# The second residual turned to token rows: 32x32 blocks on VectorE and DMAs of 128-byte runs in place of 32 transposes on TensorE

## The chip, the cores and the metric

One core of one Trainium2 chip runs the whole layer in one launch. The metric is the device time of one execution in microseconds (us), the median of the runs shown. A profile of one execution stands beside it; its span is counted from the first to the last instruction, and the positions in it (for example "at 508.29") are us from the start of the span.

The engines named below: PE is TensorE (PEld its weight loads), DVE is VectorE, ACT is ScalarE, POOL is GpSimd, SP is SyncE, which here only issues DMAs. A "q" behind an engine's name means its instruction queue.

## The reference

One macaron layer on x of 512 tokens by 1024 channels, all in float32:

```python
x = x + 0.5 * swiglu_ffn(rmsnorm(x, ffn1_norm), ffn1_w_gate, ffn1_w_up, ffn1_w_down)
x = x + hybrid_mixer(rmsnorm(x, mix_norm), w_in, q_norm, k_norm, rel_bias, pool_w, pool_scale, w_out)
x = x + 0.5 * swiglu_ffn(rmsnorm(x, ffn2_norm), ffn2_w_gate, ffn2_w_up, ffn2_w_down)
x = rmsnorm(x, final_norm)

def swiglu_ffn(x, w_gate, w_up, w_down):
    return (jax.nn.silu(x @ w_gate) * (x @ w_up)) @ w_down
```

The mixer is attention in chunks of 64 tokens and a pooling mixer side by side, then one output projection. The feed-forward width is 2816.

## The kernel before

**Number format.** Every matmul is done three times on float32r parts: an operand is split into a high part (a cast, mostly on ACT, line 130) and a low part (a subtraction on DVE, line 131). `mm3` (lines 183 to 188) multiplies high by high (L186), high by low (L187) and low by high (L188). Such a group of three matmuls is called a unit below.

**Layout.** Up to the end of the mixer, the residual is kept turned: `x[k]`, k from 0 to 7, is a tile of 128 channels by 512 tokens. The last block leaves its product by rows: 128 tokens by 512 channels. So the residual, as it stands after the mixer, is needed a second time, by rows of tokens, and is put aside in DRAM in between, in `x_d`: eight tiles (`half`, `t`) of 128 tokens by 512 channels.

**Stages.** First feed-forward block, mixer, second feed-forward block. The second one is `ffn_up` (gate and up projections), then the products of the down projection (`down2.product`). Of `ffn_up`, the first four of 22 blocks of 128 features are multiplied plainly (`PLAIN[1]` is 4), the others by a Strassen scheme with seven half-size products per block.

**The stage around the change** runs from about 480 to 570 in the span:

- The mixer ends with the output projection. `add_out(d)` (L1611, DVE) adds each of its eight column blocks to `x[d]`; `h_high`, `h_low` and `h_square` (L1620, L1629, L1640) split `x[d]` times the gain of the norm and square it; `h_sum` (L1645) adds the squares up in `acc`.
- Lines 1699 to 1708 then turn the residual: for each of the eight tiles of `x_d`, four transposes of 128x128 on PE (L1703) into one PSUM bank of the tag "a" (four banks), a copy to a tile `z` from the temporaries on ACT (L1707), and a store of 256 KB from SP (L1708).
- `ffn_up` begins with the first four blocks (two pairs of gate and up) at once: for each of four weight panels `wA[kp]` (512 KB, loaded by SP at L179 and split at L130 and L131) eight units, 32 in all, into four PSUM banks `first`. They are named kp0 to kp3 here. With the fourth panel comes `norm.finish`, at a raised priority: the sum of squares per token on PE (L304), root on ACT (L311), reciprocal on DVE, and the spread to all partitions on PE (L325), which ends in `rb` (L327, ACT).
- `evacuate` (L407 to L416) empties two of those banks: DVE multiplies the gate's bank by `rb` into a temporary `g` (L409), ACT takes the Silu into a temporary `sg` (L411), DVE multiplies by `rb` (L413) and by the up bank (L704).
- Then come the blocks of n = 2 and n = 3 (L506 to L542), 16 units each, and between them, in pieces, `norm.blocks`, which makes the operands of the Strassen products from `x` and `rb` on DVE and ACT (L350, L356, L133, L134). From L560 the order of PE, DVE and ACT is written out by hand.
- `make_sums` (L685 to L697) has POOL add weight blocks of the down projection in DRAM with DMAs (L694), a few for each block of features; each batch waits for a copy of a column that DVE has written (`mark`, L692). SP loads the first of these sums at L721.
- The rows of `x_d` are read back by `again` (L1713 to L1715), from 727.0 in the span on.

**What sets the order.** Outside the hand-written parts a planner at build time orders each engine's instructions by priority, which follows the order in the program, and puts an instruction of a later line into a gap of an earlier stage where its data and buffers are there. Each engine then runs its own list in that order. The mixer's end has an order of its own, planned by costs, but instructions of `ffn_up` can stand between it. The temporaries (`temp()`, tag "t") are eight buffers of 128x512 float32 for all users: `z`, `g`, `sg`, the squares and the diagonal of the norm.

Of the kernel before, what the change touches and what calls it, by code (L numbers as in the profile page):

```python
# [16 lines left out]
P = 128  # L17
D = 1024
S = 512
KD = D // P  # L20
NT = S // P
# [16 lines left out]
PLAIN = (5, 4)  # L38
# [16 lines left out]
def layer(  # L55
# [31 lines left out]
    nc = tc.nc  # L87
# [12 lines left out]
    def name(what):  # L100
        n_tiles[0] += 1
        return f"{what}_{n_tiles[0]}"

    def temp(dtype=F32):
        return tpool.tile([P, S], dtype, tag="t", name=name("t"))

    def bank(tag="mm", bufs=4):
        return ps.tile([P, S], F32, tag=tag, name=name(tag), bufs=bufs)

    def abank():  # L110
        return bank("a", 4)
# [61 lines left out]
    def weights(src, parts=1):  # L173
        n = src.shape[-1]
        raw = raw_tile()
        hi, lo = part_tiles()
        for i in range(parts):
            part = slice(i * n // parts, (i + 1) * n // parts)
            nc.sync.dma_start(raw[:, part], src[:, part])  # L179
            split(raw[:, part], hi[:, part], lo[:, part])  # L180
        return hi, lo

    def mm3(acc, a, b, start, stop, further=False):

        more = dict(skip_group_check=True) if further else {}
        nc.tensor.matmul(acc, a[0], b[0], start=start, stop=False, **more)  # L186
        nc.tensor.matmul(acc, a[0], b[1], start=False, stop=False, **more)  # L187
        nc.tensor.matmul(acc, a[1], b[0], start=False, stop=stop, **more)  # L188

    def cut(pair, lo, n):  # L190
        return pair[0][:, lo : lo + n], pair[1][:, lo : lo + n]


    def residual_tiles():
        pairs = [xpool.tile([P, 2 * S], F32, tag=f"x{k}", name=name("x")) for k in range(KD // 2)]
        return [pairs[k // 2][:, k % 2 * S : (k % 2 + 1) * S] for k in range(KD)]

    x = residual_tiles()
    x_d = dram.tile([2 * NT, P, S], F32, name="x_d")
# [3 lines left out]
    ident = const.tile([P, P], F32, name="ident")  # L203
# [190 lines left out]
            ]  # L394


    def ffn_up(norm, wA, down, loaded, in_order, plain):

# [6 lines left out]
        def evacuate(f, gate, up):  # L407
            g = temp()
            nc.vector.tensor_tensor(g, gate, norm.rb, op=ALU.mult)  # L409
            sg = temp()  # L410
            nc.scalar.activation(sg, g, AF.Silu)  # L411

            nc.vector.tensor_tensor(sg, sg, norm.rb, op=ALU.mult)  # L413
            down.place(f, up, sg)
            down.sums(f)
            return sg  # L416

        first = [bank() for _ in range(4)]
        for kp in range(KD // 2):
            if not loaded:  # L420
                load(2 * kp)
            w = weights(wA[kp], 1 if loaded or kp else 4)
            if not loaded:
                load(2 * kp + 1)
                norm.square(2 * kp)
                norm.square(2 * kp + 1)
            if kp == KD // 2 - 1:
                with tc.high_priority():
                    norm.finish()
            for kk in range(2):  # L430
                k = 2 * kp + kk
                for j in range(4):
                    mm3(first[j], cut(w, (kk * 4 + j) * P, P), norm.h[k], k == 0, k == KD - 1)
        evacuate(0, first[0], first[1])
        evacuate(1, first[2], first[3])
        aside = [
# [123 lines left out]
        with tc.manual_schedule(engines={E.PE, E.DVE, E.Activation}):  # L560
            last_silu = last_place = last_sums = nothing
            for n in range(plain, KF):
                f = down.order[n]
                acc, up_lo, up_hi = bank()[:, :HT], bank()[:, :HT], abank()[:, :HT]
                u, z, sg = temp(), temp(), temp()
# [71 lines left out]
    class Down:  # L637
# [76 lines left out]
        def load(self, room):  # L714

            if self.ahead:
                i, g = self.ahead.pop(0)
                raw = self.loaded[i, g] = room[:, :1024]
                src = self.rows(i, g)
                c = S if tuple(src.shape[1:]) == (groups[g][1], S) else groups[g][1] * P  # L720
                nc.sync.dma_start(raw.rearrange("p (n c) -> p n c", c=c), src)  # L721
                if room.shape[-1] > 1024:
                    self.load(room[:, 1024:])
# [85 lines left out]
    n1, n2, n3 = Norm(0), Norm(1), Norm(2)  # L809
# [19 lines left out]
    down2 = Down(list(range(KF)), lambda f: (f // 2, f % 2), block2)  # L829

    with tc.tile_pool(name="act1", bufs=1, reuse_waits="tile") as apool, ExitStack() as in_order:
        down1.begin(apool)
        ffn_up(n1, wA1, down1, False, in_order, PLAIN[0])
        x[:] = residual_tiles()
        for k in range(KD):
# [56 lines left out]
    with tc.tile_pool(name="mix", bufs=1, reuse_waits="tile") as mpool:  # L892
# [19 lines left out]
        def job(engine, cost, rank, emit, after=(), gets=(), uses=(), lag=0.0, chunk=None):  # L912
            z = Job(engine, cost, rank, emit, after, gets, uses, lag, chunk)
            z.waits = len(z.after)
            for other in z.after:
                other.then.append(z)
            for key in uses:
                held_by[key] = held_by.get(key, 0) + 1
            jobs.append(z)
            return z  # L920
# [12 lines left out]
        def part_at(slot):  # L933
# [4 lines left out]
            t=(8, lambda slot: temp()),  # L938
# [116 lines left out]
        def load_raw(i):  # L1055
            def emit():
                raw, src = buf["raw", i], sources[i]
                if len(src.shape) > 2:
                    to = raw.rearrange("p (i d k c) -> p i d k c", i=2, d=2, k=2)
                    for j in range(2):  # L1060
                        nc.sync.dma_start(to[:, j], src[:, j])
                else:
                    nc.sync.dma_start(raw, src)

            return emit
# [12 lines left out]
        for i in range(len(sources)):  # L1078
            z = job("sp", 0.4, i, load_raw(i), gets=[("raw", ("raw", i))], lag=2.0 if i < RAW else 3.6)
# [6 lines left out]
        for k, t in enumerate((7.2, 8.5, 9.7, 12.8)):  # L1086
            z = job("sp", 0.0, -9, None, lag=t)
# [46 lines left out]
        z = job("act", 1.8, -1, root_of, [z])  # L1134
        at_r = job("dve", 0.8, -1, reciprocal_root, [z], uses=["total"])
        z = job("dve", 0.65, -1, diagonal, [at_r], [("t", "diag")])
        z = job("pe", 0.9, -1, spread, [z], [("bank", "wide")], ["diag"])
# [48 lines left out]
        def pool_weights(part):  # L1186
            def emit():
                if not part:
                    w_pool.extend(
                        mpool.tile([P, S], F32R, tag=f"wp{i}", name=f"wp{i}") for i in range(2)  # L1190
                    )
                    nc.scalar.copy(w_pool[0], buf["wp"])
                else:
                    nc.vector.tensor_tensor(
                        w_pool[1], buf["wp"], w_pool[0].bitcast(F32), op=ALU.subtract
                    )

            return emit

        z = job("sp", 0.4, 5, lambda: nc.sync.dma_start(buf["wp"], wP), gets=[("t", "wp")], lag=3.6)  # L1200
        z = job("act", 0.6, RANK["wp"], pool_weights(0), [z, ready[3]])
# [407 lines left out]
        def add_out(d):  # L1609
            def emit():  # L1610
                nc.vector.tensor_tensor(x[d], x[d], buf["out", d], op=ALU.add)  # L1611

            return emit
# [36 lines left out]
        for ds, chunks in (((0, 1, 2, 3), FOUR), ((4, 5), (0, 1)), ((6, 7), (0, 1))):  # L1650
# [22 lines left out]
            for d in ds:  # L1673
                z = job("dve", 0.65, RANK["add"], add_out(d), units[d], uses=[("out", d)])
# [21 lines left out]
    with tc.tile_pool(name="act2", bufs=1, reuse_waits="tile") as apool, ExitStack() as in_order:  # L1696
        down2.begin(apool)

        for half in range(2):
            for t in range(NT):  # L1700
                tp = abank()
                for j in range(4):
                    nc.tensor.transpose(  # L1703
                        tp[:, j * P : (j + 1) * P], x[4 * half + j][:, t * P : (t + 1) * P], ident
                    )
                z = temp()
                nc.scalar.copy(z, tp)  # L1707
                nc.sync.dma_start(x_d[half * NT + t], z)  # L1708
        ffn_up(n3, wA2, down2, True, in_order, PLAIN[1])
        xt, gb = [None] * (2 * NT), [None] * 2  # L1710
        rooms[:0] = [(xpool, f"x{i}", 1, 2 * S) for i in (3, 2, 1, 0)]

# [241 lines left out]
```

## Time and profile before

| | |
|---|---|
| runs | 840.97, 841.23, 841.83 us |
| median | 841.23 us |
| the profiled execution | 840.03 us |
| its span, first to last instruction | 838.3 us |
| TensorE clock granted in it (mean) | 0.996 of full |

The profile lists busy time by engine, groups of instructions by line, the chain of work that ended last, and the DMA queues. A matmul's row gives its start and its modelled end; as matmuls are pipelined, the distance between two starts tells more than the duration. A wait is put down to the instruction that ended it.

### The profile page before, as it was taken

What the parts mean: (1) busy time and instruction counts of PE and PEld (TensorE: products, weight loads), DVE (VectorE), ACT (ScalarE), POOL (GpSimd) and SP (SyncE); (2) the same over time, 40 slices, a digit from 0 to 9 for tenths busy, and PEclk for the clock granted to TensorE, in tenths of its full rate; (3) what the DMA queues carried; (4) which work ended last, traced back from release to release, by engine and by line L of the source; (5) the groups of instructions that cost most, each with busy time, mean ns of one, the idle gap of its engine ahead of it and who ended that gap; (6) DMA issues with size and microseconds to landing.
All of it is one profiled execution on the core that took longest, in us unless ns stands there. A gap on an engine that the chain in (4) does not pass through costs nothing.

```text
span 838.3 us, 14176 instructions
## 1 busy us (share of the span) xinstructions
PE 827.9 (99%) x5332; PEld 743.9 (89%) x5332; DVE 712.1 (85%) x1115; ACT 506.0 (60%) x864; POOL 122.9 (15%) x196
## 2 busy tenths in 40 slices
PE   9999999999999999999999999999999999999996
PEld 7889999999987888888878888899999999988885
DVE  7899998999969768777699667989989999977896
ACT  8446555665757546659659545455566555756573
POOL 0013212222310000100033000111222122300010
PEclk9999999999999999999999999999999999999998
DMA  8267989889998674330311326448979889999632
GB/s 285 67 201 206 240 222 262 197 208 237 262 306 263 203 212 127 124 102 27 101 50 51 101 76 233 144 127 211 243 228 244 219 203 240 283 309 334 201 114 101
DMA packets 73828, 158.51 MB, mean 189 GB/s; under 512 B 6160, under 2 KB 31264, under 8 KB 73376
## 3 DMA queue, kind: packets, MB, share of 16 engines
q1 hardware_dynamic: 50816, 111.19, 39.1%
q0 software_dynamic: 22656, 46.14, 26.0%
q8 instruction: 42, 0.69, 0.3%
q10 hardware_dynamic: 288, 0.27, 0.1%
q14 instruction: 26, 0.21, 0.1%
HBM read 153.38 MB, written 50.34 MB: 243 GB/s over the span
## 4 chain that ended last, share of the span: by engine, by line
PE 91%; DVE 4%; DMA 3%; ACT 1%; issue 1%; DVEq 0%; ACTq 0%; SPq 0%
PE mm L186 20%; PE mm L187 20%; PE mm L188 20%; PE a L186 9%; PE a L188 9%; PE a L187 9%; DMA raw<-in_wB_dram 2%; DMA raw<-in_wA_dram 1%; DVE parts L131 1%; PE a L1546 1%; PE mm L1457 1%; PE mm L1521 1%; PE a L1521 0%; PE mm L1546 0%; PE a L219 0%
## 5 line engine op out<-in xcount | busy, mean ns | idle before, releaser
L130 ACT CAST parts<-raw 128x1024 fp32r<-128x1024 f32 (+2 forms) x77 | 74.2, 970 | 58.4 <-PE mm L187 16.2
L131 DVE TENSOR_TENSOR parts<-raw,parts 128x1024 fp32r<-128x1024 f32 (+2 forms) x77 | 85.9, 1123 | 27.6 <-ACT parts L130 27.1
L552 ACT ACTIVATE t<-mm 128x256 f32<-128x256 f32 x105 | 40.4, 385 | 114.2 <-PE mm L188 111.5
L186 PE MATMUL mm<-ha,parts 128*128 128x256 f32 x280 | 77.3, 276 | 0.0
L188 PE MATMUL mm<-ha,parts 128*128 128x256 f32 x280 | 77.3, 276 | 0.0
L187 PE MATMUL mm<-ha,parts 128*128 128x256 f32 x280 | 77.3, 276 | 0.0
L694 POOL DMA_DIRECT2D wsum<-in_wB_dram x72 | 71.8, 1153 | 35.2 <-DMA wsum<-wsum 27.6
L692 POOL COPY mark<-t 128x1 f32<-128x1 f32 x40 | 14.4, 361 | 385.0 <-DVE t L596 226.3
L463 DVE TENSOR_TENSOR parts<-wsum,parts 128x1024 fp32r<-128x1024 f32 x53 | 64.6, 1219 | 5.8 <-PE mm L188 4.3
L458 ACT CAST parts<-wsum 128x1024 fp32r<-128x1024 f32 x53 | 53.9, 1048 | 4.2 <-PE mm L187 3.9
L187 PE MATMUL mm<-parts,ah 128*128 128x512 f32 x142 | 55.5, 391 | 0.2 <-DVE parts L131 0.2
L131 DVE TENSOR_TENSOR ah<-acts,ah 128x512 fp32r<-128x512 f32 (+1 forms) x72 | 47.1, 666 | 9.7 <-ACT ah L130 9.7
L186 PE MATMUL mm<-parts,ah 128*128 128x512 f32 x142 | 55.3, 390 | 0.0
L188 PE MATMUL mm<-parts,ah 128*128 128x512 f32 x142 | 55.3, 389 | 0.0
L186 PE MATMUL mm<-hhi,parts 128*128 128x512 f32 x136 | 53.9, 400 | 0.0
L188 PE MATMUL mm<-hhi,parts 128*128 128x512 f32 x136 | 53.1, 394 | 0.0
L187 PE MATMUL mm<-hlo,parts 128*128 128x512 f32 x136 | 53.0, 391 | 0.0
L186 PEld LDWEIGHTS mm<-ha,parts 128*128 128x128 f32 x280 | 52.6, 188 | 0.1
L187 PEld LDWEIGHTS mm<-ha,parts 128*128 128x128 f32 x280 | 52.6, 188 | 0.1
L188 PEld LDWEIGHTS mm<-ha,parts 128*128 128x128 f32 x280 | 52.6, 188 | 0.0
L130 ACT CAST ah<-acts 128x512 fp32r<-128x512 f32 (+1 forms) x72 | 40.6, 580 | 13.6 <-PE mm L187 11.4
L463 DVE TENSOR_TENSOR parts<-raw,parts 128x512 fp32r<-128x512 f32 (+1 forms) x52 | 43.6, 860 | 0.6 <-ACT parts L458 0.5
(323 smaller groups left out, 2824.8 us busy)
## 6 DMA issues: line engine op xcount, KB each, us to landing
raw<-in_wA_dram SPq DMA_DIRECT2D x87, 512.0 KB, 6.1
wsum<-in_wB_dram POOLq DMA_DIRECT2D x60, 512.0 KB, 7.6
raw<-wsum SPq DMA_DIRECT2D x36, 512.0 KB, 5.7
raw<-in_wB_dram SPq DMA_DIRECT2D x30, 512.0 KB, 5.3
wsum<-wsum POOLq DMA_DIRECT2D x20, 512.0 KB, 5.2
x<-in_xT_dram SPq DMA_DIRECT2D x16, 256.0 KB, 8.8
raw<-in_wQK_dram SPq DMA_DIRECT2D x8, 512.0 KB, 3.5
wsum<-in_wB_dram POOLq DMA_DIRECT2D x12, 256.0 KB, 6.5
```

The source lines that it names most:

```text
L130: nc.scalar.copy(hi, src)
L131: nc.vector.tensor_tensor(lo, src, hi.bitcast(F32), op=ALU.subtract)
L186: nc.tensor.matmul(acc, a[0], b[0], start=start, stop=False, **more)
L187: nc.tensor.matmul(acc, a[0], b[1], start=False, stop=False, **more)
L188: nc.tensor.matmul(acc, a[1], b[0], start=False, stop=stop, **more)
L458: nc.scalar.copy(hi, src)
L463: nc.vector.tensor_tensor(lo, src, hi.bitcast(F32), op=ALU.subtract)
L552: nc.scalar.activation(dst, src, AF.Copy, scale=scale)
L692: nc.gpsimd.tensor_copy(mark[:, 0:1], after[:, 0:1])
L694: nc.gpsimd.dma_start(self.rows(i, g), self.rows(self.terms[i][at], g), **(dict(accum_op=ALU.add) if at else {}),)
L1457: nc.tensor.matmul(spot(h, t), q[a][rows, t * P : (t + 1) * P], k[b][rows, : (t + 1) * P], start=a + b == 0, stop=a == 1,)
L1521: nc.tensor.transpose(buf["tp", h, group][:, n : n + P], buf["p", h, t][:, j * P : (j + 1) * P], ident,)
```

## The change

The transposes on PE, the copies on ACT and the stores from SP are gone. `ffn_up` takes a function `put_aside`, which it calls for each `k` after the matmuls of the first four panels and before the first `evacuate`. `put_aside(k)` lets DVE turn `x[k]` (128 channels by 512 tokens) in blocks of 32x32 within the tile into a temporary `z`, so that partition 32a + q, column 32b + c of `z` holds token 32b + q of channel 32a + c. Four DMAs from POOL's queue, one for each 32 partitions, then put the blocks in their place in `x_d`: for each of 32 partitions 16 runs of 32 floats, 128 bytes each, 64 KB in all. There are 8 transposes and 32 DMAs. What `x_d` holds and who reads it is as before.

```diff
-    def ffn_up(norm, wA, down, loaded, in_order, plain):
+    def ffn_up(norm, wA, down, loaded, in_order, plain, put_aside=None):
...
                     mm3(first[j], cut(w, (kk * 4 + j) * P, P), norm.h[k], k == 0, k == KD - 1)
+        if put_aside:
+            for k in range(KD):
+                put_aside(k)
         evacuate(0, first[0], first[1])
         evacuate(1, first[2], first[3])
...
-        for half in range(2):
-            for t in range(NT):
-                tp = abank()
-                for j in range(4):
-                    nc.tensor.transpose(
-                        tp[:, j * P : (j + 1) * P], x[4 * half + j][:, t * P : (t + 1) * P], ident
-                    )
-                z = temp()
-                nc.scalar.copy(z, tp)
-                nc.sync.dma_start(x_d[half * NT + t], z)
-        ffn_up(n3, wA2, down2, True, in_order, PLAIN[1])
+        def put_aside(k):
+            z = temp()
+            nc.vector.transpose(z, x[k])
+            half, kk = divmod(k, KD // 2)
+            rows = x_d[half * NT : (half + 1) * NT].rearrange("t (b q) c -> q (t b) c", q=32)
+            for a in range(4):
+                nc.gpsimd.dma_start(
+                    rows[:, :, kk * P + a * 32 : kk * P + (a + 1) * 32],
+                    z[a * 32 : (a + 1) * 32].rearrange("q (b c) -> q b c", c=32),
+                )
+
+        ffn_up(n3, wA2, down2, True, in_order, PLAIN[1], put_aside)
```

## The prediction, made before the changed kernel was run

> **What bounds the kernel now.** I read the page first: part 1 for the busy shares, part 4 for the chain of work that ended last.
>
> ```profile
> span 838.3 us, 14176 instructions
> PE 827.9 (99%) x5332; PEld 743.9 (89%) x5332; DVE 712.1 (85%) x1115; ACT 506.0 (60%) x864; POOL 122.9 (15%) x196
> PE 91%; DVE 4%; DMA 3%; ACT 1%; issue 1%; DVEq 0%; ACTq 0%; SPq 0%
> ```
>
> PE is busy all the time and carries the chain. Work taken from PE's queue comes off the end, as long as nothing else becomes late; DVE, at 85%, is the first candidate. Then I read the place itself, in the timeline of PE (start, us, instructions).
>
> ```profile
> 502.47 0.39 PE L188 MATMUL mm<-m,parts 128*128 128x512 f32 x1
> 502.70 1.91 PE L1703 MATMUL a<-ident,x 128*128 128x128 f32 x16
> 504.36 0.48 PE L186 MATMUL mm<-hhi,parts 128*128 128x512 f32 x1
> 504.68 0.40 PE L187 MATMUL mm<-hlo,parts 128*128 128x512 f32 x1
> 504.91 0.40 PE L188 MATMUL mm<-hhi,parts 128*128 128x512 f32 x1
> 505.43 2.12 PE L1703 MATMUL a<-ident,x 128*128 128x128 f32 x16
> 507.38 1.05 PE L304 MATMUL a<-ones,acc 128*128 128x1 f32 x8
> 508.29 0.48 PE L186 MATMUL mm<-hhi,parts 128*128 128x512 f32 x1
> 509.06 0.39 PE L186 MATMUL mm<-hhi,parts 128*128 128x512 f32 x1
> 509.74 0.39 PE L186 MATMUL mm<-hhi,parts 128*128 128x512 f32 x1
> 511.33 0.39 PE L187 MATMUL mm<-hlo,parts 128*128 128x512 f32 x1
> 511.56 1.02 PE L325 MATMUL a<-t,ones 128*128 128x512 f32 x2
> 512.64 0.39 PE L186 MATMUL mm<-hhi,parts 128*128 128x512 f32 x1
> ```
>
> The mixer's last matmul starts at 502.47. Two batches of 16 transposes follow, with one unit of the first panel between them; the token sums (L304) and the second unit come at 507.38 and 508.29. A unit takes 509.74 - 509.06 = 0.68 us. So the transposes stand on PE's path, wholly uncovered.
>
> **The change part by part.**
>
> *PE.* From 502.70 to 508.29 are 5.59 us. What stays of it is one unit (0.68) and the token sums (508.29 - 507.38 = 0.91). What goes is 5.59 - 0.68 - 0.91 = **4.00 us**, with the wait for the copies' banks before 505.43. Is PE's next work ready at 502.70? The timelines of DVE and ACT say so:
>
> ```profile
> 492.92 1.23 DVE L131 TENSOR_TENSOR parts<-raw,parts 128x1024 fp32r<-128x1024 f32 x1 [0.21 <-ACT parts L130]
> 502.90 0.69 DVE L1611 TENSOR_TENSOR x<-x,mm 128x512 f32<-128x512 f32 x1 [0.49 <-PE mm L188]
> 504.11 1.22 DVE L131 TENSOR_TENSOR parts<-raw,parts 128x1024 fp32r<-128x1024 f32 x1
> 505.90 0.68 DVE L1645 TENSOR_TENSOR acc<-acc,t 128x512 f32<-128x512 f32 x1
> 512.18 1.23 DVE L131 TENSOR_TENSOR parts<-raw,parts 128x1024 fp32r<-128x1024 f32 x1 [1.85 <-ACT parts L130]
> 513.32 1.22 DVE L131 TENSOR_TENSOR wlo<-raw,whi 128x1024 fp32r<-128x1024 f32 x1
> 528.96 0.68 DVE L409 TENSOR_TENSOR t<-mm,rb 128x512 f32<-128x512 f32 x1
> ...
> 504.81 3.00 ACT L1707 COPY t<-a 128x512 f32<-128x512 f32 x6
> ```
>
> The panels kp0 to kp3 are split by 494.15, 505.33, 513.41 and 514.54. With eight units each and 0.91 for the token sums, the shortened PE asks for them at 502.70, 508.1 (502.70 + 8 x 0.68), 514.5 (502.70 + 16 x 0.68 + 0.91) and 519.9. All are there, kp2 by 1.1 us even if nothing moves. That cover is thin; were it gone, PE would wait for the rest. It should grow, for the next item.
>
> *ACT and SP.* Eight copies leave ACT (the row at 504.81 has six of them) and eight stores leave SP. Neither is on the path before; I count them as nothing. They free ACT just ahead of the cast of kp2, which is where the 1.1 us can grow.
>
> *DVE.* Eight transposes of 128x512 float32 come in; the trace has none. The nearest rows:
>
> ```profile
> L1158 DVE STREAM_SHUFFLE bias<-t 128x256 f32<-128x256 f32 x8 | 3.4, 444 | 0.0
> L409 DVE TENSOR_TENSOR t<-mm,rb 128x512 f32<-128x512 f32 x9 | 6.2, 685 | 2.3 <-ACT rb L327 2.3
> ...
> 488.70:491.30 2.60, 2.60 (x13) 2.17 (x12) 0.00 (x1) 0.00 (x0) 0.00 (x0) 1.00 0.87 252
> 496.70:500.10 3.40, 3.40 (x17) 2.82 (x16) 0.00 (x0) 0.00 (x0) 0.00 (x0) 1.00 0.08 33
> 506.60:512.10 5.50, 5.50 (x33) 4.57 (x32) 1.43 (x6) 4.81 (x10) 0.00 (x0) 1.00 0.84 317
> 512.10:541.10 29.00, 29.00 (x129) 23.82 (x128) 28.82 (x35) 11.06 (x14) 2.47 (x3) 1.00 0.40 136
> 541.10:551.40 10.30, 10.30 (x47) 8.55 (x46) 6.05 (x10) 5.39 (x8) 0.02 (x1) 1.00 0.31 103
> ```
>
> An operation of that size takes 0.685 us, and a shuffle, which also goes through blocks, 0.444 us for half the size, 0.89 for the whole at most. I take 0.69, the row of the same size: 8 x 0.69 = 5.5 us, at most 7.1. The last rows above are busy times by stretch, DVE in the fourth place: in three gaps ahead of 512.10 it stands idle for 2.6 + 3.4 + (5.5 - 1.43) = 10.1 us. x[7], the last tile, is final at 502.90 + 0.69, so the gaps can take all eight, if the planner puts them there; it did so with kp0's split at 492.92, in the middle of the mixer's end. I cost them at nothing. Without that cover they fall in a stretch in which DVE is full (28.82 of 29.00): from 512.10 to 551.40 - 4.00 = 547.40 there would be 35.30 us for 28.82 + 6.05 + 5.5 = 40.4 us of work, 5.1 us late.
>
> The Trainium skill ("VectorE: DVE Perf Modes", section "The three transpose paths") gives 390 ns for a 128x128 bf16 transpose on TensorE and 311 ns on VectorE. By that, an estimate, DVE would need 32 x 0.311 = 10.0 us where the rows say 5.5, and no longer fit the gaps with anything to spare. No run so far has the operation.
>
> *POOL.* 32 DMAs join its queue. The view of line L694, and POOL's timeline:
>
> ```profile
> L694 POOL DMA_DIRECT2D wsum<-in_wB_dram x72: 562/1144/2258, 41.1 to 741.9; - x72
> 538.63 1.12 POOL L692 COPY mark<-t 128x1 f32<-128x1 f32 x1 [78.25 <-DVE t L413]
> ...
> 708.51 0.33 SPq L721 DMA_DIRECT2D raw<-wsum  x1
> ```
>
> An issue takes 0.56 to 2.26 us, 1.14 in the middle: 32 x 1.144 = 36.6 us (18.0 to 72.3). Started at 506.6 at the latest, it ends at 543, five us into the wait that ends at 538.63 before. Behind the DMAs stand that mark and its sums; SP first asks for a sum at 708.51. Cost: nothing.
>
> *DMA engines.* 32 x 32 x 16 = 16384 runs of 128 bytes, 1024 for each of 16 engines. The DMA view of the first 3 us, and the page's row of POOL's queue, bound a run; the third row is from part 6, median us from issue to landing:
>
> ```profile
> q10 hardware_dynamic: 127, 0.01, 4.3%
> q0 software_dynamic: 22656, 46.14, 26.0%
> ...
> wsum<-in_wB_dram POOLq DMA_DIRECT2D x60, 512.0 KB, 7.6
> ```
>
> In the first, packets of 96 bytes (`gain_sb`, 24 floats for each partition) take 0.043 x 16 x 3 us / 127 = 16 ns. In the second, packets of 2 KB from DRAM to DRAM take 0.26 x 16 x 838.3 / 22656 = 154 ns. I take 16 ns, nearest in size: 1024 x 16 ns = 17 us of all engines, spread over POOL's 36.6; the upper end is 158 us. The stores of 2 MB in the same place go away, and the stretch from 512.10 on loads the engines to 0.40 (last column but one of the stretches above). Cost: nothing.
>
> *The buffers.* The eight z hold all eight temporaries until their four DMAs have landed. The first other users are the two evacuations, at 528.96 - 4.0 = 525.0 and 2 us later, with two temporaries each. By POOL's rate 8 DMAs are issued at 506.6 + 9.2 = 515.8, 16 at 524.9; with 4 us to land (an estimate: half of the 7.6 us that 512 KB need) the first evacuation is free at 520, the second at 529, 2 us late. The second one's banks are asked for only by block n = 3, 16 units (10.9 us) behind the start of n = 2, at 526.2 + 10.9 = 537. Hidden. (Block n = 2 starts at 508.29 + 31 x 0.68 + 0.86, which L325 adds between 511.33 and 512.64, = 530.2 before, and at 526.2 now.) The limit is the first evacuation: n = 2 asks for its second bank 8 units, 5.4 us, after its start, at 531.6.
>
> *What is late next.* Behind the stage the chain runs through an evacuation and a load:
>
> ```profile
> 551.42 0.57 issue
> 552.00 0.58 DVE t L409
> 557.15 8.21 DMA raw<-in_wA_dram
> ```
>
> All of it hangs on PE's end of block n = 3 at 551.4, so it moves along with PE.
>
> **Sum:** -4.00 (PE) and nothing else. The profiled execution of 840.03 us (its span is 838.3) would become 836.0; it lies 1.2 us under the median of 841.23, which becomes **837.2**.
>
> **The rivals.**
>
> 1. *DVE becomes the bound* (the transposes find no gap). For it: 28.82 of 29.00 us busy, and PE's dates come 4 us earlier. Against: 10.1 us idle just ahead, and kp2's and kp3's splits (2.4 us) can move forward into a gap too, freed by ACT. In the worst case 5.1 late: 841.23 - 4.0 + 5.1 = 842.3; with half of them in gaps, 839.6.
> 2. *The token sums are ordered too early.* PE's list is fixed at build; if L304 stands behind the first or second unit, PE waits until `acc` is done at 505.90 + 0.68 = 506.58, against 502.70 + 2 x 0.68 = 504.06: 2.5 us, 839.7. Against: before, L304 was put behind all transposes, so the planner thinks the sum late.
> 3. *The short runs are slow, and the z hold the temporaries* (slower than before). At q0's 154 ns, 256 runs per engine for the first two z take 39.4 us, so the second temporary of the first evacuation comes at 506.6 + 39.4 + 4 = 550 and PE stands from 531.6 to 550 at least, 18.4 us: 841.23 - 4.0 + 18.4 = 855.6. It decides where that temporary comes after 529.5 (531.6 less some 2 us for the Silu and two multiplications): from (529.5 - 506.6 - 4) / 256 = 74 ns per run on, or 18.9 / 8 = 2.4 us per issue. Against: 16 ns at 96 bytes, and only the slowest L694 row, 2.26, comes near the latter. The Trainium skill ("DMA: Bandwidth & Descriptors", section "Specifications") sets 512 B as the least size for line rate, with a read-modify-write below it; by that rule these runs would be this case. The trace has no writes so short.
>
> **How the numbers follow.** Forecast 64%; rival 1 14%; rival 2 10%; rival 3 12%. A measurement here tells about 0.2% (1.7 us) from no change: faster means under 839.55, slower over 842.9. Rival 1 lies within mostly, rival 2 on the edge: faster 64 + 6 = 70%, same 16%, slower 14%. The range goes from 835.0 (the forecast with its scatter and 1 us more, if kp2's earlier split also spares small stalls) to 842.6, which takes in rivals 1 and 2 and leaves out the third.
>
> **What would show it.** Right: after the mixer's last matmul, L186 follows within 0.3 us, without L1703; DVE transposes before 512; POOL's L-lines of `put_aside` end before 545. Rival 1: L409 or L463 late on DVE, and PE idle at 526 to 550. Rival 2: PE waits ahead of L304. Rival 3: L409 or L411 waiting for a DMA of z, and a DMA share near 1.0 from 506 to 545. The forecast is wrong if PE shows a new wait of over 2 us between 502 and 570.

## The result and the profile after

| | before | changed |
|---|---|---|
| median of 7 runs each | 840.97 us (839.59 to 842.17) | 838.87 us (836.84 to 839.91) |
| the profiled execution | 840.03 us | 838.87 us |
| its span | 838.3 us | 837.0 us |

The seven runs of before are the three shown above and four more. The ratio is 0.9977, 95% interval 0.9968 to 0.9987: 2.1 us faster, where 4.0 had been forecast. The busy times of the changed kernel's page (part 1), and the shares of the chain (part 4):

```profile
PE 824.5 (98%) x5300; PEld 740.9 (89%) x5300; DVE 715.7 (86%) x1123; ACT 501.8 (60%) x856; POOL 144.0 (17%) x228
PE 90%; DVE 4%; DMA 4%; ACT 1%; issue 1%; SPq 0%; DVEq 0%; ACTq 0%
```

PE has 32 instructions less and 3.4 us less of busy time. Busy time on PE is not the whole of it: in the span of 837.0 it now stands for 12.5 us, before for 10.4, and the chain passes through DMAs for 4% of the span instead of 3%. First the place of the change, in the timeline of PE:

```profile
503.71 0.39 PE L188 MATMUL mm<-m,parts 128*128 128x512 f32 x1
503.94 0.39 PE L186 MATMUL mm<-hhi,parts 128*128 128x512 f32 x1
...
508.02 0.95 PE L304 MATMUL a<-ones,acc 128*128 128x1 f32 x8
508.83 0.48 PE L186 MATMUL mm<-hhi,parts 128*128 128x512 f32 x1
...
512.10 1.02 PE L325 MATMUL a<-t,ones 128*128 128x512 f32 x2
```

The first panel's matmuls follow the mixer's last one after 0.23 us, the ordinary distance, and L304 and L325 wait for nothing. DVE and POOL have the new work there. DVE's timeline:

```profile
511.04 0.70 DVE L1704 STREAM_TRANSPOSE t<-x 128x512 f32<-128x512 f32 x1
512.90 4.27 DVE L1704 STREAM_TRANSPOSE t<-x 128x512 f32<-128x512 f32 x7
```

And POOL's:

```profile
512.04 16.11 POOL L1708 DMA_DIRECT2D x_d<-t  x25 [50.43 <-DVE t L1704]
529.15 4.50 POOL L1708 DMA_DIRECT2D x_d<-t  x7 [1.00 <-DMA x_d<-t]
```

A transpose takes 0.61 us in a row (4.27 / 7), and an issue on POOL 0.64 us (16.11 / 25). Both are cheaper than was assumed, and the DMAs are all issued by 533.65.

To see where the 4 us went, every execution is cut at three instructions of PE that all kernels have: the start of the mixer's last matmul (L188, m), the start of the first Strassen matmul (L186, xa), and PE's last matmul. The stage of the change lies between the first two.

| execution | up to the mixer's last matmul | the stage | from there to PE's last |
|---|---|---|---|
| before | 502.47 | 553.50 - 502.47 = 51.03 | 829.97 - 553.50 = 276.47 |
| changed | 503.71 | 550.64 - 503.71 = 46.93 | 828.77 - 550.64 = 278.13 |
| difference | +1.24 | **-4.10** | **+1.66** |

The first Strassen matmul, where the stage ends, in PE's timeline of before and then of the changed kernel:

```profile
553.50 0.28 PE L186 MATMUL a<-xa,parts 128*128 128x256 f32 x1
...
550.64 0.28 PE L186 MATMUL a<-xa,parts 128*128 128x256 f32 x1
```

The stage gains what was forecast. The first column has none of the change in it, so its 1.24 us is no part of the answer (another execution of the same changed kernel, below, has 501.84). The third column is the riddle: 1.66 us are given back behind the stage. There PE has one long gap; its timeline in the changed kernel shows it:

```profile
591.64 0.28 PE L188 MATMUL mm<-xa,parts 128*128 128x256 f32 x1
593.70 0.39 PE L186 MATMUL a<-ha,parts 128*128 128x256 f32 x1 [1.77 <-ACT t L555]
```

ACT's timeline shows what comes before:

```profile
592.74 0.62 ACT L461 CAST parts<-raw 128x512 fp32r<-128x512 f32 x1 [3.12 <-DMA raw<-in_wA_dram]
593.27 0.38 ACT L555 ACTIVATE t<-a 128x256 f32<-128x256 f32 x1
```

PE waits for a bank that ACT (L555) empties; ACT stands behind the cast of a weight panel (L461), and the cast waits 3.12 us for the panel's DMA. The distance between the two matmuls is 2.06 us instead of 0.11. Before, the only gap like it behind the stage was one of 0.64 us:

```profile
565.75 0.28 PE L188 MATMUL mm<-xa,parts 128*128 128x256 f32 x1
566.39 0.38 PE L186 MATMUL a<-ha,parts 128*128 128x256 f32 x1 [0.36 <-ACT t L552]
```

The chain of the changed kernel names the transfer (start, us):

```profile
581.82 10.85 DMA raw<-in_wA_dram
```

POOL's timeline names what moves beside it:

```profile
536.30 1.12 POOL L695 COPY mark<-t 128x1 f32<-128x1 f32 x1 [2.65 <-DVE t L413]
537.36 1.35 POOL L697 DMA_DIRECT2D wsum<-in_wB_dram  x2
551.87 0.58 POOL L695 COPY mark<-t 128x1 f32<-128x1 f32 x1 [13.16 <-DVE t L413]
559.07 0.25 POOL L695 COPY mark<-t 128x1 f32<-128x1 f32 x1 [6.62 <-DVE t L599]
559.61 1.79 POOL L697 DMA_DIRECT2D wsum<-in_wB_dram  x2 [0.29 <-issue]
...
579.71 0.52 POOL L697 DMA_DIRECT2D wsum<-wsum  x1 [9.55 <-DVE parts L466]
580.21 1.24 POOL L695 COPY mark<-t 128x1 f32<-128x1 f32 x1
581.40 2.09 POOL L697 DMA_DIRECT2D wsum<-in_wB_dram  x2
```

The same view of before, for comparison:

```profile
554.48 0.59 POOL L692 COPY mark<-t 128x1 f32<-128x1 f32 x1 [13.36 <-DVE t L413]
555.00 1.79 POOL L694 DMA_DIRECT2D wsum<-in_wB_dram  x2
561.08 0.24 POOL L692 COPY mark<-t 128x1 f32<-128x1 f32 x1 [4.29 <-DVE t L596]
```

Before, the second mark is followed by its two DMAs. In the changed kernel the second mark (551.87) is followed by the third (559.07), and only then by two DMAs: the second and the third batch of weight sums have slipped by one mark each in POOL's list. The fifth batch stands behind its own mark, but it comes late all the same. The last addition of the fourth batch (579.71) now stands right behind the transfer of 569.10 that it builds on, and by the trace that transfer landed at 579.42, after 10.3 us. (The row puts the wait down to L466 of DVE. In e4 and e2, two runs below, the same addition goes out 0.28 us after the landing of the same transfer, as here, 0.29, so the landing is the likelier cause.) So the two transfers of the fifth batch, 512 KB each, are issued from 581.40 on, in the same microsecond as the weight load from SP (581.82), and that load takes 10.85 us. The median of all 87 loads of its kind is 6.1 us before and 6.0 after (part 6 of the pages).

So the theory: the DMAs of the change on POOL's queue shifted the sums in the planner's order, and that costs the missing time. Its rival: the turning itself costs it, by DVE's 4.97 us (0.70 + 4.27) or by the DMAs of short runs; or it is scatter of the chip.

### The profile page after: what moved, and what is told of

It reads as the page before. It is cut to its first block, busy times and chain, and to the rows that moved or that the text cites. A ratio compares the mean times of both kernels' runs of the same rounds, so it can differ in the third digit from the quotient of the medians.

```text
span 837.0 us, 14158 instructions
## 1 busy us (share of the span) xinstructions
PE 824.5 (98%) x5300; PEld 740.9 (89%) x5300; DVE 715.7 (86%) x1123; ACT 501.8 (60%) x856; POOL 144.0 (17%) x228
## 4 chain that ended last, share of the span: by engine, by line
PE 90%; DVE 4%; DMA 4%; ACT 1%; issue 1%; SPq 0%; DVEq 0%; ACTq 0%
PE mm L186 20%; PE mm L188 20%; PE mm L187 20%; PE a L186 9%; PE a L188 9%; PE a L187 9%; DMA raw<-in_wA_dram 2%; DMA raw<-in_wB_dram 2%; DVE parts L131 1%; PE a L1549 1%; PE mm L1460 1%; PE mm L1524 1%; PE a L1524 0%; PE mm L1549 0%; DVE t L1293 0%
## 5 line engine op out<-in xcount | busy, mean ns | idle before, releaser
L555 ACT ACTIVATE t<-mm 128x256 f32<-128x256 f32 x105 | 40.3, 384 | 113.3 <-PE mm L188 110.4
L186 PE MATMUL mm<-ha,parts 128*128 128x256 f32 x280 | 77.3, 276 | 0.0
L188 PE MATMUL mm<-ha,parts 128*128 128x256 f32 x280 | 77.3, 276 | 0.0
L466 DVE TENSOR_TENSOR parts<-wsum,parts 128x1024 fp32r<-128x1024 f32 x53 | 64.5, 1218 | 5.1 <-PE mm L188 4.0
L461 ACT CAST parts<-wsum 128x1024 fp32r<-128x1024 f32 x53 | 54.0, 1049 | 3.1 <-PE mm L187 1.5
L131 DVE TENSOR_TENSOR ah<-acts,ah 128x512 fp32r<-128x512 f32 (+1 forms) x72 | 46.9, 663 | 10.3 <-ACT ah L130 10.3
L186 PE MATMUL mm<-parts,ah 128*128 128x512 f32 x142 | 55.3, 390 | 0.0
L188 PE MATMUL mm<-parts,ah 128*128 128x512 f32 x142 | 55.3, 389 | 0.0
L186 PE MATMUL mm<-hhi,parts 128*128 128x512 f32 x136 | 53.8, 400 | 0.8 <-ACT parts L130 0.8
L188 PE MATMUL mm<-hhi,parts 128*128 128x512 f32 x136 | 53.1, 394 | 0.0
L186 PEld LDWEIGHTS mm<-ha,parts 128*128 128x128 f32 x280 | 52.6, 188 | 0.1
L188 PEld LDWEIGHTS mm<-ha,parts 128*128 128x128 f32 x280 | 52.6, 188 | 0.0
L466 DVE TENSOR_TENSOR parts<-raw,parts 128x512 fp32r<-128x512 f32 (+1 forms) x52 | 43.5, 858 | 3.2 <-ACT parts L461 3.1
```

Source lines behind the costliest of these rows:

```text
L131: nc.vector.tensor_tensor(lo, src, hi.bitcast(F32), op=ALU.subtract)
L461: nc.scalar.copy(hi, src)
L466: nc.vector.tensor_tensor(lo, src, hi.bitcast(F32), op=ALU.subtract)
L555: nc.scalar.activation(dst, src, AF.Copy, scale=scale)
```

## The experiments

The first four kernels ran on one chip (before: 840.57 us, median of 17 runs), the last three on one (before: 840.37 us).

**e1: the sums back in their order.** The changed kernel, with POOL in `ffn_up` in the order of the program, which is the order of before.

```diff
-        in_order.enter_context(tc.manual_schedule(engines={mybir.EngineType.SP}))
+        pinned = {mybir.EngineType.SP} | ({mybir.EngineType.Pool} if loaded else set())
+        in_order.enter_context(tc.manual_schedule(engines=pinned))
```

> The changed kernel with one more constraint: POOL's instructions in the second block keep the order of the program, so that the second batch of weight sums is issued behind its own mark, as before the change, and not behind the third mark. PE, ACT, DVE and SP keep the changed kernel's order. Theory (the shortfall of 2 us is the wait of PE at 591.64 in the changed kernel's profile, 2.05 us, which comes of the sums being issued one batch later and landing on the weight load of 581.82): no wait of PE over 0.7 us between 565 and 600, ratio to before 0.9950 to 0.9960. Rival A (DVE is the bound, as eight transposes have come in where it is full): ratio stays at 0.9977, the wait elsewhere. Rival B (the stage gains only 2 us, the rest of the difference is scatter of the kernel's start): ratio stays at 0.9977.

Measured: 837.17 us, ratio 0.9960 (0.9947 to 0.9973). The long wait near 590 is gone. A smaller one is left at the place where before has its own. POOL's timeline in e1:

```profile
550.62 1.79 POOL L698 DMA_DIRECT2D wsum<-in_wB_dram  x2
```

The load in its chain of waits:

```profile
553.75 7.63 DMA raw<-in_wA_dram
```

And PE's timeline:

```profile
561.33 0.28 PE L188 MATMUL mm<-xa,parts 128*128 128x256 f32 x1
562.41 0.38 PE L186 MATMUL a<-ha,parts 128*128 128x256 f32 x1 [0.80 <-ACT t L556]
```

Nothing but POOL's order differs from the changed kernel: the traces of the two have the same instructions in the same order on PE, DVE, ACT and SP. So the distance in time is its price: by medians 838.13 (e4, below) - 837.17 = 1.0 us on this chip. The ratio lies at the upper edge of what was expected (0.9950 to 0.9960). The ratios' intervals overlap a little; the trace is plainer than the times here: the distance of 2.06 us near 591 in the changed kernel is gone, and one of 1.08 has come at 561.

**e2: the reverse.** The kernel before, with nothing of the change but its order of the sums.

```diff
-            part = self.steps[n * at // KF : n * (at + 1) // KF]
+            cut_at = lambda j: self.steps[n * j // KF : n * (j + 1) // KF]
+            part = cut_at(at)
+            if self.block is block2 and at in (1, 2, 3):
+                part = {1: [], 2: cut_at(1), 3: cut_at(3)[:1] + cut_at(2) + cut_at(3)[1:]}[at]
```

> The kernel before, with nothing changed but the place of two batches of weight sums in POOL's queue: the second batch stands behind the third mark and the third behind the fourth, exactly as the planner put them in the changed kernel. Theory: a wait of PE of 1 to 2.5 us appears near 590 to 600 and the ratio to before is 1.001 to 1.003. Rivals A and B: POOL is off the path, the ratio is 1.000.

Measured: 845.33 us, ratio 1.0057 (1.0045 to 1.0070): the right direction and much more than expected. The load takes 13.00 us by the chain:

```profile
585.28 13.00 DMA raw<-in_wA_dram
```

PE waits twice as long as in the changed kernel (timeline):

```profile
595.10 0.28 PE L188 MATMUL mm<-xa,parts 128*128 128x256 f32 x1
599.30 0.39 PE L186 MATMUL a<-ha,parts 128*128 128x256 f32 x1 [3.93 <-ACT t L552]
```

The busy times by stretch go on from there, with the granted clock in the last column but two:

```profile
599.20:603.00 3.80, 3.69 (x21) 3.70 (x22) 3.73 (x7) 0.33 (x2) 0.00 (x0) 0.64 0.44 168
603.00:608.00 5.00, 5.00 (x43) 5.00 (x42) 4.00 (x7) 3.86 (x6) 2.32 (x3) 0.93 0.30 36
```

After a distance of 4.20 us without a matmul the granted clock is 0.64 for 3.8 us and 0.93 for 5.0 more. At full clock that is 3.8 x 0.36 + 5.0 x 0.07 = 1.7 us of lost work on top of the wait. The two together, 4.2 - 0.64 + 1.7 = 5.3 us, come near the 281.64 - 276.47 = 5.17 us by which this kernel's third column exceeds that of before. Here too the order of PE, DVE, ACT and SP is the same as before. So the shifted sums are harmful by themselves, without any turning.

**e3: no turning.** e1 without the transposes on DVE. The 32 DMAs read `x[k]` as it is. This takes more away than the transposes: the DMAs no longer wait for DVE and start at 480 instead of 510, and the planner also orders PE, ACT and DVE anew in the stage.

```diff
-            z = temp()
-            nc.vector.transpose(z, x[k])
+            z = x[k]
```

> As the first run (sums in order), but the eight transposes on DVE are left out and the 32 DMAs take the tiles of the residual as they are, so the rows put aside are not the right ones. This prices the DVE work alone. Theory: DVE's 4.9 us cost PE 0.3 us at most, the ratio is within 0.0005 of the first run's. Rival A: the ratio is lower by 0.002 or more.

Measured: 836.20 us, ratio 0.9951 (0.9939 to 0.9963), 0.0009 under e1: more than the 0.0005 expected, and well short of the 0.002 of rival A. The stage takes 549.33 - 502.40 = 46.93 us, in e1 548.87 - 501.94 = 46.93: with or without eight transposes on DVE, the same to a hundredth. What is left of DVE's cost lies behind the stage (third column 276.75 in e3, 277.14 in e1). The load that PE waits for is issued 552.98 - 549.33 = 3.65 us behind the first Strassen matmul in e3 and 553.75 - 548.87 = 4.88 us in e1, because DVE is later with the split that frees its buffer (before, it was also 557.15 - 553.50 = 3.65 us). DVE's timeline in e3 has the split at

```profile
551.37 1.22 DVE L467 TENSOR_TENSOR wlo<-raw,whi 128x1024 fp32r<-128x1024 f32 x1
```

and in e1, where the stage ended 0.46 us earlier, at

```profile
552.09 1.22 DVE L467 TENSOR_TENSOR wlo<-raw,whi 128x1024 fp32r<-128x1024 f32 x1
```

By these two traces the transposes, with the order that comes with them, cost some 0.4 us of PE's time (277.14 - 276.75), by this detour. The difference of the two medians, 1.0 us, is larger and isn't clear of their scatter (e7, the same kernel as e1, is 0.0005 above e3), so the size of this cost stays rough.

**e4: the changed kernel again**, on the chip of e1 to e3.

> The changed kernel again, beside the others on one chip. All theories: ratio 0.997 to 0.9985. Theory: a wait of PE of 1.5 to 2.5 us near 590, as in the first profile; rival B: the difference between its gain in the stage (about 4.1 us) and in the whole lies ahead of 15 us.

Measured: 838.13 us, ratio 0.9974 (0.9961 to 0.9987), as the first time. Its profiled execution reaches the mixer's last matmul at 501.84 where the first one had 503.71, so that part is scatter. The stage is 46.93 us again. The load takes 9.82 us this time (10.85 the first), the distance on PE is 1.03 us (2.06), short of the 1.5 to 2.5 expected, and the third column 277.08 us (278.13): the wait scatters by a microsecond with the load. This profiled execution, at 835.96 us, was the fastest of the twelve of this kernel (up to 842.99), and by its columns nothing sets it apart from e1's. The medians do, and the first trace. The cost of the shifted sums rests on those, and on e2, where they are alone.

**e5: the second batch early.** e1 with the second batch of sums issued right behind the first. Two weight loads move there too (issued 539.04 and 539.42), but PE does not wait for them.

```diff
+            cut_at = lambda j: self.steps[n * j // KF : n * (j + 1) // KF]
+            part = cut_at(at)
+            if self.block is block2 and at in (0, 1):
+                part = {0: cut_at(0) + cut_at(1), 1: []}[at]
```

> As e1_sums_in_order, and the two DMAs of the second batch of weight sums follow the first batch directly on POOL, at about 537, instead of waiting for the second mark at 550. Nothing else in any engine's order differs from e1. Theory (the weight load that PE waits for next is slow only while a batch of sums moves beside it): the load issued at about 553.8 in e1 has the DMA engines to itself and takes 6 us or less instead of 7.6; PE's wait of 1.08 us near 561 shrinks to under 0.5; ratio to before about 0.0007 under e1's, 0.9945 to 0.9960. Rival (loads take that long whatever runs beside them, the date comes from ACT or DVE): the load still takes over 7 us, PE's wait stays over 0.9, ratio as e1's.

Measured: 836.16 us, ratio 0.9947 (0.9933 to 0.9961), the lowest of all. POOL's timeline:

```profile
535.92 1.35 POOL L701 DMA_DIRECT2D wsum<-in_wB_dram  x2
540.15 1.80 POOL L701 DMA_DIRECT2D wsum<-in_wB_dram  x2 [2.88 <-DMA wsum<-in_wB_dram]
```

The load, in SP's:

```profile
554.08 0.55 SPq L455 DMA_DIRECT2D raw<-in_wA_dram  x1
```

Its cast, in ACT's:

```profile
560.01 0.62 ACT L462 CAST parts<-raw 128x512 fp32r<-128x512 f32 x1
```

And PE's:

```profile
561.65 0.28 PE L188 MATMUL mm<-xa,parts 128*128 128x256 f32 x1
561.76 0.28 PE L186 MATMUL a<-ha,parts 128*128 128x256 f32 x1
```

ACT's cast waits for nothing, so the load took less than 560.01 - 554.08 = 5.93 us, against 7.63 in e1; by its landing in the trace it took 5.4. The first trace of the changed kernel says the same: there the second batch goes out at 559.61 only, and the load issued at 555.52 took 5.2 us. PE's distance is 0.11: no wait at all. The third column is 825.24 - 549.20 = 276.04 us, 0.43 under before, near the size of the wait that before has at 566 (0.64 - 0.11 = 0.53). The rival expectation (the load takes that long whatever runs beside it) falls.

**e6: the 32 DMAs from SP's queue.** The changed kernel with one word exchanged, and POOL's order left to the planner.

```diff
-                nc.gpsimd.dma_start(
+                nc.sync.dma_start(
```

> The changed kernel with the 32 DMAs of put_aside on SP's queue instead of POOL's; POOL's order is left to the planner. By the build's order the second batch of sums then stands behind the second mark again, as before the change. Theory (the DMAs on POOL's queue are what moved the sums by a mark): no load of over 9 us and no wait of PE of over 1.5 us at 585 to 595; ratio to before 0.9945 to 0.9970, near that of e1. Rival (the sums' place is not what costs the 2 us): ratio 0.9970 to 0.9985, as the changed kernel's. SP's queue carries the weight loads, so 32 issues there may delay the load behind them; the planner's order on PE, ACT and DVE also differs from e1's from about 590 on, so this run is less clean than e1.

Measured: 842.08 us, ratio 1.0021 (1.0010 to 1.0031). Half of the theory held: the second batch stands behind the second mark again, and no wait of over 1.5 us is left at 585 to 595. So it is the DMAs' being on POOL's queue that moves the sums. The ratio missed by far, as a new wait takes the place of the old. SP's timeline in e6:

```profile
510.16 18.28 SPq L1708 DMA_DIRECT2D x_d<-t  x32
528.54 0.45 SPq L179 DMA_DIRECT2D raw<-in_wA_dram  x1
```

ACT's:

```profile
537.64 1.05 ACT L130 CAST sa<-aside 128x1024 fp32r<-128x1024 f32 x1 [4.64 <-DVE aside L356]
543.30 0.63 ACT L411 ACTIVATE t<-t 128x512 f32<-128x512 f32 x1 [4.62 <-DVE t L409]
543.84 1.03 ACT L130 CAST whi<-raw 128x1024 fp32r<-128x1024 f32 x1
```

And PE's:

```profile
542.09 0.39 PE L188 MATMUL mm<-hhi,parts 128*128 128x512 f32 x1
544.92 0.50 PE L186 MATMUL mm<-hhi,whi 128*128 128x512 f32 x1 [2.44 <-ACT whi L130]
```

A weight load stands behind the 32 issues on SP and goes out at 528.54; in e1 it does at 511.24. The planner, which saw it late, put its cast on ACT behind an L411 that needs PE's block to be finished. ACT stands idle from 538.69 to 543.30 for that L411, and PE then for the cast. The load itself landed 4.0 us after its issue, so its data had long been there; the order is the likely cause, which no run tested by itself. Once a temporary is also waited for, the sign that the prediction set for its third rival: ACT's first L411 of the stage (524.97) waits 3.38 us for a DMA of `z`. PE shows no wait there.

**e7: e1 again**, beside e5 and e6.

> e1_sums_in_order once more, on the same chip as the two runs beside it: ratio to before 0.9947 to 0.9973 if the first result holds; the measured reference for the other two.

Measured: 836.59 us, ratio 0.9956 (0.9943 to 0.9969); stage 46.93 us, third column 277.22. e1's result holds. Between e7 and e5 the medians are only 0.43 us apart, which the times alone don't tell from nothing; the traces do (277.22 against 276.04 us, a distance of 1.17 against 0.11).

All runs by their columns, with the longest distance between two matmuls behind the stage:

| execution | stage | to PE's last | longest distance | median ratio |
|---|---|---|---|---|
| before | 51.03 | 276.47 | 0.64 at 566 | 1 |
| changed | 46.93 | 278.13 | 2.06 at 592 | 0.9977 |
| e4, changed again | 46.93 | 277.08 | 1.03 at 590 | 0.9974 |
| e1, sums in order | 46.93 | 277.14 | 1.08 at 561 | 0.9960 |
| e7, the same again | 46.93 | 277.22 | 1.17 at 561 | 0.9956 |
| e3, no turning | 46.93 | 276.75 | 0.94 at 562 | 0.9951 |
| e5, second batch early | 46.98 | 276.04 | 0.24 at 769 | 0.9947 |
| e2, before, sums late | 51.05 | 281.64 | 4.20 at 595 | 1.0057 |
| e6, DMAs from SP | 50.48 | 279.32 | 1.37 at 554 | 1.0021 |

Less what this distance has over the ordinary 0.11 us, the third column is 275.9 to 276.2 us in all but the last two rows: one wait explains the column. In e2 the clock adds its share, and e6 has several waits.

## Why the prediction came out as it did

- **PE, -4.00.** Right: the stage became 4.05 to 4.10 us shorter in every run with the 32 DMAs on POOL's queue. The units were asked for as planned, and kp2 was split well in time, by 508.42 + 1.22 = 509.64.
- **DVE, at nothing.** Nearly right in size, half right in its reason. The eight took 4.97 us, near the 5.5 that the prediction took from its rows and half of the 10.0 of its other estimate. The prediction wanted them in the gaps ahead of 512; the planner put one at 511.04 and seven from 512.90, into the stretch called full. The gaps filled up all the same, with the splits of kp2 and kp3: they started at 512.18 and 513.32 before and do at 508.42 and 511.76 now. The prediction had named that as a point against rival 1. Still the stage didn't grow (e3 has the same 46.93 us). Rival 1 had priced the case at up to 5.1 us, by adding all of DVE's work up to the stage's end. But DVE had time to spare up to that end. Here are the busy times of the whole stage, in before and then in the changed kernel, DVE in the fourth place:

```profile
502.47:553.50 51.03, 50.91 (x248) 42.18 (x247) 42.09 (x57) 27.19 (x40) 2.49 (x3) 1.00 0.44 155
...
503.71:550.64 46.93, 46.93 (x216) 38.83 (x215) 45.23 (x64) 22.72 (x31) 23.02 (x35) 1.00 0.61 169
```

DVE stood idle for 51.03 - 42.09 = 8.94 us of the stage before and does for 1.70 now, and PE waits for none of its work there. What is left of the price shows behind the stage, as a load issued 1.23 us later (e3 against e1), some 0.4 us.

- **POOL: "Behind the DMAs stand that mark and its sums; SP first asks for a sum at 708.51. Cost: nothing."** This is the step that failed. Its size was too careful (0.64 us per issue against 1.144, the end at 533.65 against 543). Its reading was off too: 543 is not "into the wait that ends at 538.63" but past it, so by its own figures the mark and the first sums would have come late. But the main fault lies in the question. It asked who waits for the sums' result, and nobody does until 708. It didn't ask what the sums do on their way: two transfers of 512 KB beside a weight load that PE waits for. And it took POOL's order behind the DMAs as given, though the planner makes that order anew.
- **"All of it hangs on PE's end of block n = 3 at 551.4, so it moves along with PE."** Wrong for the same reason. The load of 8.21 us that stands in the quoted chain is a load beside the second batch (issued 555.00, the load 557.15). It was the sign that a load here takes longer when sums move beside it, and that it has no slack. Moved sums make another load 10.85 us long, and e5 shows that this one takes 5.4 with the sums out of its way.
- **The short runs.** Cheap enough, as forecast. Here is the row of POOL's DMA queue in the DMA view of the changed kernel from 508 to 537, where it carries nothing else:

```profile
q0 software_dynamic: 1024, 2.10, 39.6%
```

The 32 DMAs landed 2.3 to 5.9 us after their issue, 3.4 in the middle. The 16384 runs took 0.396 x 16 x 29 us = 184 us of an engine's time, 11 ns each (the forecast took 16). The trace counts 32 of them as one packet of 4 KB. In e6, from SP's queue, it lists them one by one, 16384 packets of 128 bytes at 13 ns. That is not the rate of long runs: a packet of 4 KB took 0.35 us here, and one of the weight loads beside it 0.16 us in the middle. This kernel could afford it. The Trainium skill ("DMA: Bandwidth & Descriptors", section "Specifications") has a read-modify-write below 512 B, and 512 B as the least size for line rate. The lower rate agrees with that; whether there was a read-modify-write, no trace shows. The prediction's "no writes so short" in the trace was not so: the 96-byte packets that it priced at 16 ns go into partitions of `gain_sb`. Rival 3, which needed 74 ns a run, is out, and nobody but POOL itself (1.0 us) waited for the landing of these DMAs.

- **Rival 2** is out: L304 at 508.02 follows the unit before it at the ordinary distance.
- **The sign of being wrong** was set as "a new wait of over 2 us between 502 and 570". The wait came at 592, beyond the window that was looked at: the order changed in the stage, and the bill came 40 us behind it.

In sum: -4.10 in the stage as forecast (-4.00), and behind it 1.66 given back, of which the longer wait is 2.06 - 0.64 = 1.42. That leaves -2.44 by the first profiled execution, and -4.10 + 0.61 = -3.49 by the second (e4). The medians are -2.10 and 838.13 - 840.57 = -2.44, so most executions probably had a wait like the first; how it is spread over them the two traces can't tell. On the chip of e1 the account nearly closes: of the 4.10 - 2.44 = 1.66 us that are missing, 0.96 go when the sums are back in order (838.13 - 837.17), and 0.67 is what e1's third column still gives back (277.14 - 276.47). With the sums put early the change is worth 840.37 - 836.16 = 4.21 us (e5), of which some 0.4 is the wait that before has of its own. By time alone e5 is not clear of e1, e7 and e3.

## What to carry to other kernels

When work joins a queue, look at what stands behind it in that queue for what it does while it runs, not only for who needs its result: background transfers lengthen the loads beside them. A planner makes every order anew, so after such a change compare the order of each engine with that of before, well past the stage that was edited. And where the chain of waits already runs through a load of more than the usual length, treat that load as without slack, and ask what moves beside it.

## What the runs showed of the hardware

- After a distance of 4.20 us without a matmul (e2) the granted clock was 0.64 for the next 3.8 us and 0.93 for 5.0 us more. After one of 2.06 us (the changed kernel) it stayed at full:

```profile
593.70:597.50 3.80, 3.80 (x33) 3.80 (x34) 3.73 (x7) 0.96 (x3) 0.00 (x0) 1.00 1.03 402
```

After one of 2.83 us (e6, 542.09 to 544.92) it stayed at full as well, 1.00 over the next 3.8 us. The Trainium skill ("TensorE: Matmul & The Clock Gate", section "What's actually happening") has the clock at half after an idle window of about 3.4 us; the three runs agree with it. The wait of e2 cost more than itself, by 1.7 us on top of 4.2.

- A load of 512 KB, the second of a pair, took 5.2 us (changed, issued 555.52) and 5.4 us (e5, 554.08) with no sum issued in its first four us, 7.63 (e1) with a batch of sums issued 2.5 us ahead of it, and 10.85 (changed, 581.82) and 13.00 us (e2) with the late batches around it.
- An issue of a DMA with 512 runs took 0.64 us on POOL (16.11 / 25) and 0.57 us on SP (18.28 / 32, e6). The cheaper queue gave the slower kernel, by the trace for the load that stood behind the issues.
- 16384 runs of 128 bytes from tiles to DRAM took 11 ns each from POOL's queue (changed) and 13 ns from SP's (e6).
- A transpose of 128x512 float32 in blocks of 32x32 on DVE took 0.61 us in a row, near the 0.69 us of an ordinary operation of that size.
